# Stacked halves of q and k placed by DMA, outputs of a pair of heads added at once, reciprocals for three blocks at once

## The chip, the cores and the metric

The kernel runs on one core of one Trainium2 chip. The metric is the device time of one execution in microseconds (us).

## What is computed

Two transformer blocks on 512 rows of width 1024 in float32, the output of the first being the input of the second. The first is one layer with three branches of 8 heads of 64 each: A is attention with a relative bias, B a gated recurrence, C attention with a part of q and k turned by position. The second has two layers, each with 8 heads of forgetting attention, 8 heads of retention, a gated convolution and a gated extra input. Of all this the change touches the heads:

```python
def forgetting_attention(q, k, v, f_logit):
    ...
        logits = jnp.einsum('bhqd,bhkd->bhqk', qb, k).astype(jnp.float32) * scale
        logits = logits + cq[..., :, None] - cum[..., None, :]
        qpos = start + jnp.arange(Q_BLOCK)
        logits = jnp.where(kpos[None, :] <= qpos[:, None], logits, -jnp.inf)
        probs = jax.nn.softmax(logits, axis=-1)
        return jnp.einsum('bhqk,bhkd->bhqd', probs.astype(v.dtype), v)

def chunkwise_retention(q, k, v, log_gamma):
    ...
        scores = jnp.einsum('bhid,bhjd->bhij', qc, kc) * intra_decay
        inner = jnp.einsum('bhij,bhje->bhie', scores, vc)
        cross = jnp.einsum('bhid,bhde->bhie', qc, state) * q_decay[:, :, None]
```

Branch A's heads are the forgetting heads with a bias by distance in place of the decay and a mask by chunks of 64; the kernel computes retention over all 512 rows at once, with a table of decays over the lower triangle.

## The kernel before

**Layout.** Activations are held as channels x rows: a tile is 128 x 512, 128 channels (two heads) by all 512 rows. Every float32 operand of a matmul is split into a high half of type fp32r (a rounded copy) and a low half (what is left), and a product takes three matmuls: high by high, low by high, high by low. The dense products (`lin`, line 503; the tile is `lin` in the profile) do this with 128 x 512 outputs and make up most of the work of TensorE.

**Who sets the order.** Nothing is ordered by hand. The host runs all pieces of work as generators in a planner (`Net`, line 248; `drive`, line 301), each with a priority, lower first, and the order in which they issue is the order of the program on each engine. The planner has a clock `now` of TensorE's work, which goes on with each matmul (128 x 512: 215.8 ns), and a guess of when VectorE, ScalarE and GpSimd are done with what they have (`Eng`, line 211): VectorE 75 + 1.042 ns for each column, ScalarE 100 + 0.84, GpSimd 165 + 0.84, each a bit more for operands that are one per partition. A piece that waits for an engine yields `w()`, the guessed end plus 200 ns. DMAs by SyncE have no cost in it; a piece that waits for one yields a fixed time (`HD` 3700 ns for the exchange of rows in the rotary product, `SD` 3000 ns for tables). The stream of dense products has priority 20 and fills TensorE whenever no head is due. Roles (`take`, `give`) hold back what may run at once: `Q` (2) is the number of pairs that hold stacks, `R` (2) the number of retention pairs, `S` and `T` the attention heads in their scores and in their outputs, `sc`, `po` and `pt` are the PSUM tiles of scores, outputs and transposes.

**Weights.** SyncE's queue loads weights in program order into three buffers `raw` (line 426); ScalarE makes the high half `wh`, VectorE the low half `wl`, and the next load is issued when `wl` is planned. The same queue carries, in program order, everything else that SyncE issues.

**Heads.** `heads` (line 1052) runs a pair of attention heads in A and in the layers, `ret` (line 1716) a pair of retention heads, `hgrn` (line 1250) a pair of branch B. For both kinds of q and k that stand as a pair in one tile, `stack` (line 802, 20 times: 4 in A, 8 in each layer) builds three operands for each head e of the pair: `qd` has the high half of q in both blocks of 64 partitions, `ks` has the high half of k in the head's own block and the low half in the other, and `ql` has the low half of q in one block and zeros in the other. So two matmuls over 128 partitions, qd by ks and ql by ks, give the scores of a head. ScalarE copies q (`qh`), half of k into `ks` and half of qh into `qd`; GpSimd copies the other half into `qd` and sets half of `ql` to zero; VectorE does four subtractions of 64 x 512. `soft` (line 865) makes the probabilities P of a block of 128 rows: bias and least value (VectorE), exponential with the sum over the row (ScalarE), reciprocal of the sum (VectorE), scaling (GpSimd). The four blocks of P are then transposed (`pt`), split into `ph` and `pl`, and `pv` (line 777) multiplies them with the values. The result po (128 x 512, in PSUM) has two parts in its two blocks of 64 partitions, which `pvout` (line 792) adds: ScalarE copies one part across the blocks (`tl`), VectorE adds it to the other, straight from PSUM, into this head's half of `y`. 56 heads do this: 8 each in A, B and C, 16 in each layer.

**The rotary product** (`rotary`, line 1692; q and k of retention pairs) writes `ra` on VectorE, exchanges its blocks of 32 partitions into `rb` by four DMAs from SyncE's queue, then multiplies `ra` on GpSimd and `rb` on VectorE by tables and adds the two on VectorE.

In the profile the operations of VectorE, ScalarE and GpSimd stand at line 221 (`Eng`), matmuls at 379, transposes at 389, loads of weights at 432, the exchange of rows at 1703. In names of tiles, `lg` is a score with its bias, `m` its least value, `st` a retention score with its decay `dec`.

Of the kernel before, what the change touches and what calls it, by code (L numbers as in the profile page):

```python
# [8 lines left out]
F32 = mybir.dt.float32  # L9
F32R = mybir.dt.float32r  # L10
# [3 lines left out]
AF = mybir.ActivationFunctionType  # L14
ALU = mybir.AluOpType
# [5 lines left out]
TUNE = dict(  # L21
    NG=66,
    NTRI=5,
    MARGIN=8,
    MQ=4,
    R=2,
    Q=2,
    S=1,
    T=1,
    LAT=200.0,  # L30
    HD=3700.0,
    SD=3000.0,
    LATPOS=3,
# [7 lines left out]
NT = S // 128  # L41
# [206 lines left out]
class Net:  # L248
# [543 lines left out]
    def pvout(self, h, po, y, yev):  # L792
        nc = self.nc
        a, b = (slice(0, 64), slice(64, 128)) if h % 2 == 0 else (slice(64, 128), slice(0, 64))
        tl = yield from self.g("tl")
        self.ac.activation(tl[a], po[b], AF.Copy)
        yield self.w("ac")
        self.dv.tensor_tensor(out=y[a], in0=po[a], in1=tl[a], op=ALU.add)
        self.free(po, tl)
        self.sig(yev, "dv")  # L800

    def stack(self, q, k):


        qh = yield from self.g("qh", F32R)
        self.ac.activation(qh, q.h, AF.Copy)
        qd, ks, ql = [], [], []
        for e in range(2):
            r, o = slice(64 * e, 64 * e + 64), slice(64 - 64 * e, 128 - 64 * e)
            ks.append((yield from self.g("ks", F32R)))  # L810
            self.ac.activation(ks[e][r], k.h[r], AF.Copy)
            ql.append((yield from self.g("ql", F32R)))
            self.pl.memset(ql[e][o].bitcast(F32), 0.0)
        yield self.w("ac")
        for e in range(2):
            r, o = slice(64 * e, 64 * e + 64), slice(64 - 64 * e, 128 - 64 * e)
            self.dv.tensor_tensor(out=ks[e][o], in0=k.h[r], in1=ks[e][r].bitcast(F32), op=ALU.subtract)
            qd.append((yield from self.g("qd", F32R)))
            self.pl.tensor_scalar(out=qd[e][r], in0=qh[r].bitcast(F32), scalar1=1.0, scalar2=1.0, op0=ALU.mult, op1=ALU.mult)
            self.ac.activation(qd[e][o], qh[r].bitcast(F32), AF.Copy)  # L820
        for e in range(2):
            r = slice(64 * e, 64 * e + 64)
            self.dv.tensor_tensor(out=ql[e][r], in0=q.h[r], in1=qh[r].bitcast(F32), op=ALU.subtract)
        self.free(qh, q.h, k.h)
        yield self.w("dv", "gp", "ac")
        return [[(qd[e], ks[e]), (ql[e], ks[e])] for e in range(2)], [[qd[0], ks[0], ql[0]], [qd[1], ks[1], ql[1]]]

    def head(self, h, qk, vs, y, yev, bias, mask, qdone, hdone):

        nc = self.nc  # L830
        yield from self.take("S", 1, TUNE["S"])
        P = yield from self.tri("P")
        po = (0, 128, 384, 768, 1280)
        pev = [Ev() for _ in range(NT)]
        for i in range(NT):
            w = 128 * (i + 1)
            ps = yield from self.psr("sc", 2, "sc")
            for j, (q, k) in enumerate(qk):
                self.mm(ps[:, :w], q[:, 128 * i:w], k[:, :w], j == 0, mask is None and j == len(qk) - 1)
            if mask is not None:  # L840
                self.mm(ps[:, 128 * i:w], self.idb, mask, False, True)
            self.spawn(self.soft(ps, w, P[:, po[i]:po[i + 1]], bias, pev[i]), 0)
            yield 300.0
# [6 lines left out]
        evs = [Ev() for _ in range(NT)]  # L850
        at = self.AT
        yield pev[NT - 1]
        for j in range(NT):
# [10 lines left out]

    def soft(self, ps, w, p, bias, ev):
        nc = self.nc
        m = self.sm(1, "m")
# [11 lines left out]
        yield self.w("dv")  # L879
        sm = self.sm(1, "sum")  # L880
        self.ac.activation(p, src, AF.Exp, bias=m, scale=-1.0, accum_out=sm)
        self.free(tmp)
        yield self.w("ac")
        r = self.sm(1, "r")
        self.dv.reciprocal(r, sm)
        yield self.w("dv")
        self.pl.tensor_scalar(out=p, in0=p, scalar1=r, scalar2=1.0, op0=ALU.mult, op1=ALU.mult)
        self.sig(ev, "gp")

# [162 lines left out]
    def heads(self, pr, q, k, vs, y, mk, mask, prio=2):  # L1052
# [6 lines left out]
        else:  # L1059
            qk, used = [[(q[e].h[q[e].s], k[e].h[k[e].s])] for e in range(2)], [[q[e].h, k[e].h] for e in range(2)]  # L1060
        t = yield from self.g("y")
        e2 = [Ev(), Ev()]
# [17 lines left out]
        yield e2[1]  # L1080
        yield from self.split(t, y)

# [167 lines left out]
    def hgrn(self, pr, q, z, gz, vs, y):  # L1250
        nc = self.nc
# [71 lines left out]
        self.give("Bl")  # L1323
        yv = yield from self.g("y")
        yev = [Ev(), Ev()]
        yield vs.ev
        for e in range(2):
            yield done[e]
            yield from self.pv(2 * pr + e, vs, hi[e], lo[e], None, yv, yev[e])
            self.free(hi[e], lo[e])  # L1330
            self.after(vs, 1)
# [384 lines left out]
    def ret(self, pr, q, k, gz, vs, y):  # L1716
# [11 lines left out]
        qk, used = yield from self.stack(q, k)  # L1728
        yv = yield from self.g("yr")
        yield max(0.0, there - self.now)  # L1730
        yev = [Ev(), Ev()]
        for e in range(2):
# [14 lines left out]
            if e:  # L1747
                self.give("Q")
            yield from self.pv(h, vs, ph, pl, evs, yv, yev[e])
            self.free(ph, pl, dec)  # L1750
# [459 lines left out]
```

## Time and profile before

| what | us |
| --- | --- |
| median of 3 runs (from, to) | 2324.69 (2324.03, 2325.5) |
| the profiled execution | 2324.91 |
| its span, first to last instruction | 2323.2 |
| TensorE (PE) busy | 2278.9 (98%) |
| VectorE (DVE) busy | 1518.4 (65%) |
| ScalarE (ACT) busy | 1067.4 (46%) |
| GpSimd (POOL) busy | 479.0 (21%) |
| mean granted TensorE clock | 0.994 of full speed |

How to read it: the span is from the first to the last instruction of the one execution that was recorded; the time of that execution also has what lies around the span. Busy is the time in which an engine executes instructions; two matmuls that overlap in the pipeline count once. PE is TensorE with its matmuls, SP is SyncE with its DMA queue. The span falls into branch A (to about 170 us), C and B (to about 500), the merging and the feed-forward of the first block (to about 940), the heads of the second block's first layer (about 1000 to 1150), its dense part (to about 1700), the second layer's heads (about 1700 to 1850) and its dense part.

### The profile page before, as it was taken

To read this page: it belongs to the slowest core of one execution; us is meant where nothing else is said; L and a number is where in the kernel's file an instruction comes from. 1 tells how busy PE (TensorE), PEld (TensorE's weight loads), DVE (VectorE), ACT (ScalarE), POOL (GpSimd) and SP (SyncE) were. 2 spreads that over 40 slices of the span, in tenths; PEclk is the share of its full clock that TensorE was granted. 3 is DMA by queue.
4 is the path that set the end of the run, shared out by engine and by line. 5 is a ranking of instruction groups with operands and counts; after the bars stand their busy time and mean duration, and the time that the engine had idled before them with its cause. 6 is when DMAs were issued, how large, how long until landed. Compare 5 with 4: busy or idle time off the path is not lost.

```text
span 2323.2 us, 29048 instructions
## 1 busy us (share of the span) xinstructions
PE 2278.9 (98%) x10810; PEld 1868.2 (80%) x10810; DVE 1518.4 (65%) x2375; ACT 1067.4 (46%) x1695; POOL 479.0 (21%) x571
## 2 busy tenths in 40 slices
PE   9999999999999999999999999999999999999998
PEld 6887877778888888887878888888887878888887
DVE  6878499976542554679975652457688866652466
ACT  4767466664322233466643331245556544332343
POOL 3523044431000002334430000002425320000012
PEclk9999999999999999999999999999999999999999
DMA  5321322123332222433333233323432332233332
GB/s 178 87 74 55 91 73 64 56 87 116 98 100 97 94 100 84 155 95 101 119 105 100 93 98 100 102 91 115 125 108 90 118 109 92 99 100 93 107 95 69
DMA packets 75727, 228.24 MB, mean 98 GB/s; under 512 B 9664, under 2 KB 15680, under 8 KB 75584
## 3 DMA queue, kind: packets, MB, share of 16 engines
q1 hardware_dynamic: 70400, 209.62, 28.2%
q0 software_dynamic: 5184, 16.75, 2.5%
q8 instruction: 85, 1.39, 0.3%
q14 instruction: 58, 0.48, 0.1%
HBM read 215.29 MB, written 6.32 MB: 95 GB/s over the span
## 4 chain that ended last, share of the span: by engine, by line
PE 87%; DVE 8%; issue 2%; POOL 1%; ACT 1%; DMA 0%; SPq 0%; POOLq 0%; DVEq 0%; ACTq 0%
PE lin L379 73%; PE v L379 5%; PE sc L379 3%; PE po L379 3%; DVE wl L221 2%; PE pt L389 2%; DVE xl L221 1%; DVE dg L221 1%; DVE eq L221 0%; DVE ks L221 0%; DVE pre L221 0%; DVE qk L221 0%; DVE ql L221 0%; DVE sl L221 0%; DVE suf L221 0%
## 5 line engine op out<-in xcount | busy, mean ns | idle before, releaser
L379 PE MATMUL lin<-xh,wh 128*128 128x512 f32 (+1 forms) x2752 | 1088.0, 395 | 0.0
L379 PE MATMUL lin<-xl,wh 128*128 128x512 f32 (+1 forms) x2752 | 1072.3, 390 | 6.7 <-DVE xl L221 6.7
L379 PE MATMUL lin<-xh,wl 128*128 128x512 f32 (+1 forms) x2728 | 1061.5, 389 | 0.0
L221 DVE TENSOR_TENSOR wl<-raw,wh 128x1024 fp32r<-128x1024 f32 (+3 forms) x391 | 468.9, 1199 | 500.8 <-PE lin L379 329.3
L221 ACT ACTIVATE wh<-raw 128x1024 fp32r<-128x1024 f32 (+4 forms) x394 | 392.4, 996 | 807.7 <-PE lin L379 659.8
L379 PEld LDWEIGHTS lin<-xl,wh 128*128 128x128 f32 x2752 | 517.3, 188 | 117.8 <-DVE xl L221 8.8
L379 PEld LDWEIGHTS lin<-xh,wh 128*128 128x128 f32 x2752 | 518.0, 188 | 105.0 <-issue 3.5
L379 PEld LDWEIGHTS lin<-xh,wl 128*128 128x128 f32 x2728 | 514.4, 189 | 96.7
L221 POOL TENSOR_TENSOR sq<-sq 128x512 f32<-128x512 f32 (+1 forms) x61 | 90.1, 1477 | 566.6 <-ACT sq L221 565.9
L221 POOL MEMSET pad<- 128x2 f32 x44 | 4.4, 99 | 586.3 <-DVE cv L221 586.3
L221 POOL TENSOR_SCALAR P<-P,r 128x128 f32<-128x128 f32 (+3 forms) x128 | 86.5, 681 | 149.3 <-DVE r L221 133.0
L221 DVE SCALAR_TENSOR_TENSOR cv<-pad,vec,cv 128x512 f32<-128x512 f32 x88 | 66.1, 752 | 40.7 <-ACT cv L221 39.0
L379 PE MATMUL v<-wh,xh 128*128 128x512 f32 x192 | 78.3, 408 | 0.7 <-POOL wh L221 0.7
L379 PE MATMUL v<-wl,xh 128*128 128x512 f32 x192 | 75.9, 395 | 3.1 <-DVE wl L221 3.1
L379 PE MATMUL v<-wh,xl 128*128 128x512 f32 x192 | 75.7, 394 | 0.0
L221 ACT ACTIVATE ph<-pt 128x512 fp32r<-128x512 f32 (+3 forms) x128 | 55.6, 435 | 42.2 <-PE pt L389 40.8
L221 DVE TENSOR_TENSOR x<-lin,x 128x512 f32<-128x512 f32 x80 | 54.6, 683 | 23.5 <-PE lin L379 23.5
L221 DVE TENSOR_TENSOR pl<-pt,ph 128x512 fp32r<-128x512 f32 (+3 forms) x128 | 60.2, 479 | 12.7 <-ACT ph L221 12.2
L221 ACT ACT_TABLE_LOAD x51 | 65.4, 1283 | 4.2 <-DVE qk L221 1.6
L221 ACT ACTIVATE P<-lg,m 128x128 f32<-128x128 f32 (+1 forms) x96 | 53.6, 558 | 28.9 <-DVE m L221 21.9
L221 ACT ACTIVATE tl<-po 64x512 f32<-64x512 f32 x56 | 33.2, 592 | 73.1 <-PE po L379 72.6
L221 DVE CUSTOM_DVE_ANT_0 lg<-sc,E 128x128 f32<-128x128 f32 (+1 forms) x96 | 45.6, 483 | 31.9 <-PE sc L379 23.1
(244 smaller groups left out, 2578.1 us busy)
## 6 DMA issues: line engine op xcount, KB each, us to landing
raw<-wup SPq DMA_DIRECT2D x88, 512.0 KB, 3.3
raw<-w SPq DMA_DIRECT2D x83, 512.0 KB, 3.6
raw<-wf SPq DMA_DIRECT2D x64, 512.0 KB, 3.3
raw<-wdn SPq DMA_DIRECT2D x32, 512.0 KB, 3.5
raw<-wv SPq DMA_DIRECT2D x22, 512.0 KB, 3.6
raw<-wpg SPq DMA_DIRECT2D x16, 512.0 KB, 3.3
raw<-wbr SPq DMA_DIRECT2D x12, 512.0 KB, 3.3
raw<-wdn SPq DMA_DIRECT2D x16, 384.0 KB, 3.1
```

The lines of the kernel that those rows point to most:

```text
L221: r = f(*a, **k)
L379: self.nc.tensor.matmul(out, l, r, start=start, stop=stop)
L389: self.nc.tensor.transpose(out, src, self.ident)
```

## The change

Three edits, and a constant for the planner.

*Stacks.* ScalarE copies all of q and all of k (two tiles `sph`), VectorE takes both low halves with full tiles (two tiles `spl`), and twelve DMAs of 64 rows from SyncE's queue place the halves: six of `sph` (both blocks of each qd, the own block of each ks), then six of `spl` (the other block of each ks, both blocks of each ql). ql has the low half of q in both blocks now, where one was zero. The second batch is issued by the planner after the subtractions, and 5000 ns (`ST`) after that the stack counts as ready.

*Outputs.* ScalarE copies both parts of po, one across the blocks into a shared tile `y.l`, one straight into `y.h`; po is then free, and the second head of the pair to come triggers one add of two full tiles on VectorE.

*Reciprocals.* The sums of the four blocks go to columns of one tile. Blocks 0 and 1 end with the exponential; block 2 takes the reciprocals of three columns at once, and the three scalings follow on GpSimd; block 3 is as before. Transposes wait for both.

```diff
+    ST=5000.0,
...
     def pvout(self, h, po, y, yev):
         a, b = (slice(0, 64), slice(64, 128)) if h % 2 == 0 else (slice(64, 128), slice(0, 64))
-        tl = yield from self.g("tl")
-        self.ac.activation(tl[a], po[b], AF.Copy)
+        if y.l is None:
+            y.l = yield from self.g("tl")
+        self.ac.activation(y.l[a], po[b], AF.Copy)
+        self.ac.activation(y.h[a], po[a], AF.Copy)
+        self.sig(yev, "ac")
+        y.s += 1
         yield self.w("ac")
-        self.dv.tensor_tensor(out=y[a], in0=po[a], in1=tl[a], op=ALU.add)
-        self.free(po, tl)
-        self.sig(yev, "dv")
+        self.free(po)
+        if y.s == 2:
+            self.dv.tensor_tensor(out=y.h, in0=y.h, in1=y.l, op=ALU.add)
+            self.free(y.l)
+            self.sig(yev, "dv")
...
     def stack(self, q, k):
-        qh = yield from self.g("qh", F32R)
-        self.ac.activation(qh, q.h, AF.Copy)
-        qd, ks, ql = [], [], []
+        h, l, qd, ks, ql = [], [], [], [], []
+        for x in (q, k):
+            h.append((yield from self.g("sph", F32R)))
+            l.append((yield from self.g("spl", F32R)))
+            self.ac.activation(h[-1], x.h, AF.Copy)
         for e in range(2):
-            r, o = slice(64 * e, 64 * e + 64), slice(64 - 64 * e, 128 - 64 * e)
             ks.append((yield from self.g("ks", F32R)))
-            self.ac.activation(ks[e][r], k.h[r], AF.Copy)
+            qd.append((yield from self.g("qd", F32R)))
             ql.append((yield from self.g("ql", F32R)))
-            self.pl.memset(ql[e][o].bitcast(F32), 0.0)
         yield self.w("ac")
-        for e in range(2):
-            r, o = slice(64 * e, 64 * e + 64), slice(64 - 64 * e, 128 - 64 * e)
-            self.dv.tensor_tensor(out=ks[e][o], in0=k.h[r], in1=ks[e][r].bitcast(F32), op=ALU.subtract)
-            qd.append((yield from self.g("qd", F32R)))
-            self.pl.tensor_scalar(out=qd[e][r], in0=qh[r].bitcast(F32), scalar1=1.0, scalar2=1.0, op0=ALU.mult, op1=ALU.mult)
-            self.ac.activation(qd[e][o], qh[r].bitcast(F32), AF.Copy)
-        for e in range(2):
-            r = slice(64 * e, 64 * e + 64)
-            self.dv.tensor_tensor(out=ql[e][r], in0=q.h[r], in1=qh[r].bitcast(F32), op=ALU.subtract)
-        self.free(qh, q.h, k.h)
-        yield self.w("dv", "gp", "ac")
+        for j, x in enumerate((q, k)):
+            self.dv.tensor_tensor(out=l[j], in0=x.h, in1=h[j].bitcast(F32), op=ALU.subtract)
+
+        def dma(out, in_):
+            self.nc.sync.dma_start(out=out.bitcast(F32), in_=in_.bitcast(F32))
+
+        rows = [(slice(64 * e, 64 * e + 64), slice(64 - 64 * e, 128 - 64 * e)) for e in range(2)]
+        for e, (r, o) in enumerate(rows):
+            for d in (r, o):
+                dma(out=qd[e][d], in_=h[0][r])
+            dma(out=ks[e][r], in_=h[1][r])
+        yield self.w("dv")
+        for e, (r, o) in enumerate(rows):
+            dma(out=ks[e][o], in_=l[1][r])
+            for d in (r, o):
+                dma(out=ql[e][d], in_=l[0][r])
+        self.free(*h, *l, q.h, k.h)
+        yield TUNE["ST"]
...
     def head(self, h, qk, vs, y, yev, bias, mask, qdone, hdone):
...
+        yield pev[NT - 2]
         yield pev[NT - 1]
...
     def soft(self, ps, w, P, po, i, sums, r, bias, pev):
...
-        self.ac.activation(p, src, AF.Exp, bias=m, scale=-1.0, accum_out=sm)
+        self.ac.activation(P[:, po[i]:po[i + 1]], src, AF.Exp, bias=m, scale=-1.0, accum_out=sums[:, i:i + 1])
         self.free(tmp)
         yield self.w("ac")
-        r = self.sm(1, "r")
-        self.dv.reciprocal(r, sm)
+        if i < NT - 2:
+            return
+        js = range(NT - 1) if i == NT - 2 else [i]
+        self.dv.reciprocal(r[:, js[0]:js[-1] + 1], sums[:, js[0]:js[-1] + 1])
         yield self.w("dv")
-        self.pl.tensor_scalar(out=p, in0=p, scalar1=r, scalar2=1.0, op0=ALU.mult, op1=ALU.mult)
-        self.sig(ev, "gp")
+        for j in js:
+            p = P[:, po[j]:po[j + 1]]
+            self.pl.tensor_scalar(out=p, in0=p, scalar1=r[:, j:j + 1], scalar2=1.0, op0=ALU.mult, op1=ALU.mult)
+        self.sig(pev[i], "gp")
```

Since the planner's costs change with these lines, the order moves too.

SyncE's queue at the first retention pairs of the first layer. Before, weights (`raw`) alternate with exchanges of rows (`rb2<-ra`):

```order
L432 DMA raw_8956<-w2 128x1024
L1703 DMA rb2_8962<-ra_8961 32x512 x4
L432 DMA raw_9034<-w2 128x1024
L1703 DMA rb2_9040<-ra_9039 32x512 x4
L432 DMA raw_9090<-w2 128x1024
L432 DMA raw_9140<-w2 128x1024
L432 DMA raw_9211<-w2 128x1024
L1703 DMA rb2_9217<-ra_9216 32x512 x4
```

And now, from the second batch of the retention pair's stack on:

```order
L433 DMA raw_9026<-w2 128x1024
L825 DMA ks_8994<-spl_8992 64x512
L825 DMA ql_8996<-spl_8989 64x512 x2
L825 DMA ks_8997<-spl_8992 64x512
L825 DMA ql_8999<-spl_8989 64x512 x2
L825 DMA qd_9058<-sph_9051 64x512 x2
L825 DMA ks_9057<-sph_9054 64x512
L825 DMA qd_9061<-sph_9051 64x512 x2
L825 DMA ks_9060<-sph_9054 64x512
L433 DMA raw_9085<-w2 128x1024
...
L1725 DMA rb2_9100<-ra_9099 32x512 x4
```

The exchange for the next pair's q (rb2_9217 before, rb2_9100 now) stands behind the twelve DMAs of the retention pair's stack, those of the next forgetting pair's stack and two weights.

VectorE's queue at the same place, around the product with the exchanged rows (`rb<-rb,rot`). Before:

```order
L221 TENSOR_TENSOR pl<-st,ph 128x128
L221 ISA lg,m<-sc,E 128x128
L221 ISA m 128x1
L221 ISA lg,m<-sc,E 128x256
L221 ISA m 128x1
L221 TENSOR_TENSOR rb_9217<-rb_9217,rot 128x512
L221 ISA lg,m<-sc,E 128x384
L221 ISA m 128x1
```

And now:

```order
L222 TENSOR_TENSOR st<-sc,dec 128x128
L222 TENSOR_TENSOR pl<-st,ph 128x384
L222 TENSOR_TENSOR pl<-st,ph 128x256
L222 TENSOR_TENSOR pl<-st,ph 128x128
L222 TENSOR_TENSOR rb_9100<-rb_9100,rot 128x512
L222 TENSOR_TENSOR st<-sc,dec 128x512
L222 TENSOR_TENSOR ra<-ra,rb_9100 128x512
L222 TENSOR_TENSOR st<-sc,dec 128x384
```

The product stood between the scores of an attention head, and stands now ahead of the `st` of the second retention head.

## Rows read from the trace of the kernel before

**Rows 1.** The page, part 1: busy us (share) and instructions by engine.

```profile
PE 2278.9 (98%) x10810; PEld 1868.2 (80%) x10810; DVE 1518.4 (65%) x2375; ACT 1067.4 (46%) x1695; POOL 479.0 (21%) x571
```

**Rows 2.** Windows: us, busy us (instructions) by engine, granted clock, DMA share, GB/s.

```profile
300.00:500.00 200.00, 186.06 (x1121) 145.34 (x1122) 186.39 (x286) 132.75 (x189) 86.30 (x67) 0.99 0.21 64
500.00:940.00 440.00, 439.97 (x1955) 363.98 (x1951) 217.04 (x264) 139.47 (x172) 34.13 (x30) 1.00 0.30 98
1050.00:1150.00 100.00, 96.42 (x499) 78.96 (x498) 92.40 (x188) 62.01 (x125) 50.24 (x58) 1.00 0.30 93
1750.00:1850.00 100.00, 96.21 (x491) 79.08 (x490) 89.21 (x183) 62.10 (x125) 47.47 (x53) 0.98 0.31 98
```

**Rows 3.** Waits of PE from 1050 to 1150 us: us in total, times, longest.

```profile
PE pt L389 <- POOL P L221: 2.0, 3, 1.3
PE po L379 <- DVE pl L221: 1.1, 2, 0.7
```

**Rows 4.** Groups by line: what the change removes or alters.

```profile
L221 DVE TENSOR_TENSOR ks<-qk,ks 64x512 fp32r<-64x512 f32 x24 | 18.9, 788 | 0.9 <-ACT ks L221 0.4
L221 DVE TENSOR_TENSOR ks<-ra,ks 64x512 fp32r<-64x512 f32 x16 | 12.9, 809 | 1.5 <-ACT ks L221 1.1
L221 DVE TENSOR_TENSOR ql<-qk,qh 64x512 fp32r<-64x512 f32 x24 | 18.4, 766 | 0.3
L221 DVE TENSOR_TENSOR ql<-ra,qh 64x512 fp32r<-64x512 f32 x16 | 11.6, 724 | 0.3
L221 POOL TENSOR_SCALAR qd<-qh 64x512 fp32r<-64x512 f32 x40 | 31.3, 783 | 29.1 <-ACT qh L221 27.5
L221 POOL MEMSET ql<- 64x512 f32 x40 | 20.8, 520 | 1.8
L221 ACT ACTIVATE qh<-qk 128x512 fp32r<-128x512 f32 x12 | 7.4, 620 | 0.0
L221 ACT ACTIVATE tl<-po 64x512 f32<-64x512 f32 x56 | 33.2, 592 | 73.1 <-PE po L379 72.6
L221 DVE TENSOR_TENSOR y<-po,tl 64x512 f32<-64x512 f32 x40 | 27.4, 685 | 9.8 <-ACT tl L221 9.3
L221 DVE RECIPROCAL r<-sum 128x1 f32<-128x1 f32 x128 | 18.8, 154 | 4.7 <-ACT P L221 4.1
```

**Rows 5.** Groups by line: an add of two full tiles in SBUF.

```profile
L221 DVE TENSOR_TENSOR xl<-y,xh 128x512 fp32r<-128x512 f32 x16 | 11.1, 695 | 0.0
```

**Rows 6.** Timeline of the SP queue: start us, us, issues.

```profile
1030.72 2.43 SPq L1703 DMA_DIRECT2D rb<-ra  x4
1035.61 0.33 SPq L432 DMA_DIRECT2D raw<-w  x1
1056.56 2.41 SPq L1703 DMA_DIRECT2D rb<-ra  x4
```

**Rows 7.** Tile rb: landing times of the DMAs that exchange halves of rows.

```profile
DMA to landing us min/median/max: 2.0/2.5/3.7
```

**Rows 8.** Timeline of ACT: copies of q and k of two retention pairs.

```profile
1041.71 0.62 ACT L221 ACTIVATE qh<-ra 128x512 fp32r<-128x512 f32 x1
1045.10 1.29 ACT L221 ACTIVATE ks<-ra 64x512 fp32r<-64x512 f32 x2 [2.77 <-DVE ra L221]
1048.80 0.63 ACT L221 ACTIVATE qh<-qk 128x512 fp32r<-128x512 f32 x1
...
1074.04 0.62 ACT L221 ACTIVATE qh<-ra 128x512 fp32r<-128x512 f32 x1
```

**Rows 9.** Timeline of PE: first scores of the same two retention pairs.

```profile
1051.38 0.39 PE L379 MATMUL sc<-qd,ks 128*128 128x512 f32 x1
...
1079.85 0.39 PE L379 MATMUL sc<-qd,ks 128*128 128x512 f32 x1
```

**Rows 10.** Timeline of DVE: the rotary product that needs the exchanged rows.

```profile
1061.34 1.24 DVE L221 TENSOR_TENSOR rb<-rb,rot 128x512 f32<-128x512 f32 x1
```

**Rows 11.** Timeline of POOL: three scalings of probabilities.

```profile
1066.16 5.93 POOL L221 TENSOR_SCALAR P<-P,r 128x256 f32<-128x256 f32 x3
```

More of the change, by code (lines that the diff above doesn't have):

```diff
@@ L834, in head @@
         pev = [Ev() for _ in range(NT)]
+        sums, r = self.sm(NT, "sum"), self.sm(NT, "r")
         for i in range(NT):
@@ L841, in head @@
                 self.mm(ps[:, 128 * i:w], self.idb, mask, False, True)
-            self.spawn(self.soft(ps, w, P[:, po[i]:po[i + 1]], bias, pev[i]), 0)
+            self.spawn(self.soft(ps, w, P, po, i, sums, r, bias, pev), 0)
             yield 300.0
@@ L863, in head, with soft @@
         hdone()
-    def soft(self, ps, w, p, bias, ev):
-        nc = self.nc
+    def soft(self, ps, w, P, po, i, sums, r, bias, pev):
         m = self.sm(1, "m")
@@ L879, in soft @@
         yield self.w("dv")
-        sm = self.sm(1, "sum")
-        self.ac.activation(p, src, AF.Exp, bias=m, scale=-1.0, accum_out=sm)
+        self.ac.activation(P[:, po[i]:po[i + 1]], src, AF.Exp, bias=m, scale=-1.0, accum_out=sums[:, i:i + 1])
         self.free(tmp)
         yield self.w("ac")
-        r = self.sm(1, "r")
-        self.dv.reciprocal(r, sm)
+        if i < NT - 2:
+            return
+        js = range(NT - 1) if i == NT - 2 else [i]
+        self.dv.reciprocal(r[:, js[0]:js[-1] + 1], sums[:, js[0]:js[-1] + 1])
         yield self.w("dv")
-        self.pl.tensor_scalar(out=p, in0=p, scalar1=r, scalar2=1.0, op0=ALU.mult, op1=ALU.mult)
-        self.sig(ev, "gp")
+        for j in js:
+            p = P[:, po[j]:po[j + 1]]
+            self.pl.tensor_scalar(out=p, in0=p, scalar1=r[:, j:j + 1], scalar2=1.0, op0=ALU.mult, op1=ALU.mult)
+        self.sig(pev[i], "gp")
     def hilo(self, ps, h, l, ev, after=None):
@@ L1060, in heads @@
             qk, used = [[(q[e].h[q[e].s], k[e].h[k[e].s])] for e in range(2)], [[q[e].h, k[e].h] for e in range(2)]
-        t = yield from self.g("y")
+        t = X(0)
+        t.s = 0
+        t.h = yield from self.g("y")
         e2 = [Ev(), Ev()]
@@ L1080, in heads @@
         yield e2[1]
-        yield from self.split(t, y)
+        yield from self.split(t.h, y)
     def branch_a(self, N, ya, C):
@@ L1323, in hgrn @@
         self.give("Bl")
-        yv = yield from self.g("y")
+        yp = X(0)
+        yp.s = 0
+        yv = yp.h = yield from self.g("y")
         yev = [Ev(), Ev()]
@@ L1328, in hgrn @@
             yield done[e]
-            yield from self.pv(2 * pr + e, vs, hi[e], lo[e], None, yv, yev[e])
+            yield from self.pv(2 * pr + e, vs, hi[e], lo[e], None, yp, yev[e])
             self.free(hi[e], lo[e])
@@ L1728, in ret @@
         qk, used = yield from self.stack(q, k)
-        yv = yield from self.g("yr")
+        yp = X(0)
+        yp.s = 0
+        yv = yp.h = yield from self.g("yr")
         yield max(0.0, there - self.now)
@@ L1748, in ret @@
                 self.give("Q")
-            yield from self.pv(h, vs, ph, pl, evs, yv, yev[e])
+            yield from self.pv(h, vs, ph, pl, evs, yp, yev[e])
             self.free(ph, pl, dec)
```

1 line of the change is left out of this document (removed).

## The prediction, made before the changed kernel was run

> **What bounds the kernel now.** I read the page's busy times first, then windows of stages, then what PE waits for, then the groups that the change touches, and last the timelines of SP, ACT, PE, DVE and POOL around one retention pair. TensorE is busy for 2278.9 of 2323.2 us [rows 1], so 44.3 us is all that anything off TensorE could give back. Where only dense layers run, nothing is left: from 500 to 940 us TensorE is busy for 439.97 of 440 us [rows 2]. The change adds and removes no matmul, so it can act only where TensorE stands still beside heads. Three windows show that [rows 2]: branch B (300 to 500 us) with 200 - 186.06 = 13.9 us of standing, the end of the first layer's heads (1050 to 1150) with 100 - 96.42 = 3.6 us, and the same place in the second layer (1750 to 1850) with 3.8 us. The last also has a mean granted clock of 0.98, which over 100 us is 2 us at most. In the same 100 us VectorE is busy for 92.4 and 89.2 us, more than it is anywhere else in a layer, and TensorE's waits there are 2.0 us for probabilities P that GpSimd scales and 1.1 us for pl of VectorE [rows 3]. So a gain there must come from VectorE's or GpSimd's queue getting shorter; branch A and branch C have no standing worth counting.
>
> The profiled execution took 2324.91 us, 0.22 us over the median of 2324.69. I sum against it and take the 0.2 us off at the end. About 0.2% (4.6 us) is what a measurement of this kernel can tell from no change.
>
> **The change part by part.**
>
> *Stacks (20 of them).* VectorE loses 40 subtractions for ks (18.9 + 12.9 = 31.8 us) and 40 for ql (18.4 + 11.6 = 30.0 us) [rows 4] and gets 40 of full tiles; a subtraction of two full tiles in SBUF takes 695 ns [rows 5], so 27.8 us. That is -34 us. GpSimd loses 31.3 us of qd and 20.8 us of memsets, -52 us [rows 4]. ScalarE has a full copy of q and four half copies today, and two full copies then; at 0.62 us each [rows 4, 8] that is 100 against 40, -37 us. SyncE gets 12 more DMAs for each stack, 240 in all.
>
> *Outputs (56 heads, 28 pairs).* VectorE's 56 adds at 685 ns (38 us) become 28 of full tiles at 695 ns (19.5 us): -19 us. ScalarE copies both parts, 56 more copies at 592 ns: +33 us [rows 4, 5]. ScalarE is busy for 62 of 100 us in the end of a layer [rows 2], so I cost them at nothing; without that cover a copy of 0.59 us would stand before the next pv of each head. The buffer po is free after ScalarE now, not after VectorE.
>
> *Reciprocals.* 128 become 64, 64 x 154 ns = -10 us [rows 4]. The scaling of the first three blocks of P starts only with the third sum; GpSimd then has three scalings in a row before the fourth.
>
> *What of this reaches TensorE.* In the 100 us at the end of a layer's heads stand about six stacks, five pairs of outputs and four attention heads. VectorE is relieved there by 6 x (4 x 0.76 - 2 x 0.695) = 9.9, by 5 x 0.675 = 3.4 and by 4 x 2 x 0.154 = 1.2 us: 14.5 of 92.4 us. The upper bound of the gain is all the standing and the clock's loss, 3.6 + 3.8 + 2.0 = 9.4 us. The lower bound is nothing, because the planner knows that VectorE has less to do and sets the matmuls closer by as much; only the part of a wait that its costs did not see can go. I take a bit over half, **-5.0 us**, because the two kinds of wait named in [rows 3] both sit behind the relieved queues. In branch B only the outputs change: 8 adds at 0.685 become 4 at 0.695 us, -2.7 us on a VectorE that is busy for 186 of 200 us [rows 2]. The order of the last pair's work moves there too, so the bounds are -2.7 and +3 (a quarter of the 13.9 us for a denser order, taken as an estimate from that row), and I take **-0.5 us**.
>
> *The new wait: SyncE.* The trace has no DMA of 64 rows within SBUF. The nearest row is the exchange of rows for the rotary product: four DMAs of 32 rows take 2.43 us of the queue, 0.61 us each; the other end is a weight load at 0.33 us [rows 6]. They land 2.5 us after issue in the median, 3.7 at most [rows 7]. I take 0.61 us, since that is a move within SBUF from one block of partitions to another, as these are. A stack then takes 12 x 0.61 = 7.3 us of SyncE, in two batches of six.
>
> (a) Are the operands late? A retention pair's first scores need nine of the twelve DMAs: 2 x 0.62 us of copies, 8 x 0.61 = 4.9 us to the start of the ninth, 2.5 us to land, 8.6 us together. The room today is 1051.38 - 1041.71 = 9.7 us for the first pair and 1079.85 - 1074.04 = 5.8 us for the second [rows 8, 9]. The planner grows it: it counted 1590 + 200 + 2432 + 200 = 4.4 us and now counts 1060 + 200 + 1216 + 200 + 5000 = 7.7 us, 3.3 us more. So 13.0 and 9.1 us against 8.6: just in time. With the longest landing (3.7 us) the tight pair would be 0.7 us late. Bounds 0 and 8 pairs x 0.4 = 3 us; I take **+0.5 us**.
>
> (b) What stands behind them in SyncE's queue? Weight loads, which have room, and the exchange of rows for the next rotary product. At the first retention pair of a layer the order on SyncE is now stack, stack of a forgetting pair, exchange. k of the first pair is ready at 1045.10 and its copy done at 1045.7 [rows 8]; from there four DMAs of its first batch (2.4), a weight (0.3), its second batch (3.7), the other stack's first batch (3.7), a weight (0.3) and its second batch (3.7) end at 1059.8, where the exchange was issued at 1056.56 [rows 6]. It then lands at 1059.8 + 3 x 0.61 + 2.5 = 1064.1. VectorE began the product with the exchanged rows at 1061.34 [rows 10], without a wait. So **VectorE would stand 2.8 us** at the head of its queue, with the st and pl of the second retention head right behind it, for which TensorE's scores and outputs wait. With 0.33 us an issue, the two stacks end before 1056, and nothing is late. Bounds 0 and 2.8 us in each of two layers; I count half, as TensorE's place is not fixed to VectorE's: **+3.0 us**.
>
> Sum: -5.0 - 0.5 + 0.5 + 3.0 = -2.0 us, 2322.9 us for a profiled execution and **2322.7 us** for the median: no change that can be told.
>
> **Rule against row.** GpSimd's three scalings of P from 1066.16 on took 5.93 us together, while VectorE ran through a dense row of operations [rows 11], and this is the wait of TensorE in [rows 3]. The Trainium skill (SBUF — State Buffer, section Who interferes with whom) says that a VectorE instruction with two SBUF inputs and a GpSimd instruction that reads SBUF exclude each other for a whole instruction. That rule speaks against one part of the change: the outputs' add had one input in PSUM and now has both in SBUF. The row of an add of two SBUF tiles says 0.695 against 0.685 us, a loss of 0.3 us over 28 adds, and that is what my sum has.
>
> **The rivals.**
>
> 1. *Slower: the SyncE queue.* If an issue costs 0.61 us or more, the exchange lands late by the whole 2.8 us in both layers and TensorE feels all of it (5.6 us), and the tight retention pairs are late by 0.4 us each (3 us), while a quarter of the gain is left (-2 us): +6.6 us, 2331 us. It decides from about 0.5 us an issue. For it: the row of [rows 6] and the room of 0.5 us in (a). Against it: the weights in the same queue show 0.33 us, and VectorE has less to do before it gets to the product, or more behind it that isn't urgent. Chance 0.24.
>
> 2. *Faster: the relief counts in full.* The 14.5 us off VectorE's 92.4 us remove nearly all standing in both layers (-7.4 to -9.4 us) and half of B's 2.7 us: about -8.5 us, 2316 us, at best 2312. For it: 92.4 us in 100 is a full queue, and TensorE waits only for its results. Against: the planner packs the order closer by the same amount. Chance 0.36.
>
> 3. *Nothing: GpSimd and VectorE lock each other.* The full adds and subtractions of two SBUF tiles meet the three scalings that now follow each other, and P is as late as before; the waits of [rows 3] stay, the rest cancels: 2324.5 us. For it: 5.93 us for three scalings. Against: 40 copies of qd on GpSimd go, and 80 subtractions become 40. This is how the rule above would work here. Chance 0.10.
>
> **How the numbers follow.** The forecast has 0.30, and with rival 3 (0.10) no change has 0.40; faster 0.36 is rival 2, slower 0.24 is rival 1. The range runs from rival 2 at its best (2312) to rival 1 with a little over its price (2332). No change, the likeliest alone, would be 2320 to 2327.
>
> **What would show it.** Right: VectorE down by some 60 us and GpSimd by some 50 us in all, 240 more issues on SyncE at about 0.6 us, standing of TensorE in the layers' last 100 us of heads down from 3.6 and 3.8 to about 2 us, a wait of VectorE for rb of one to three us in each layer. Wrong: a first matmul of scores that waits for ks or ql by more than 0.5 us, weights that wait for their load, standing in branch B that moves by more than 3 us, or an issue cost of 0.4 us or less.

## The result, and the profile after

The changed kernel takes 2352.5 us (median of 4 runs, 2350.1 to 2353.9) against 2324.8 us before: a ratio of 1.0118 with a 95% interval of 1.0103 to 1.0132, 27.7 us slower. The forecast was 2322.7 us and no change, and the range ended at 2332. The profiled execution took 2350.09 us, the fastest of the four. Its page, part 1, beside [rows 1]:

```profile
PE 2290.5 (98%) x10810; PEld 1872.8 (80%) x10810; DVE 1466.4 (62%) x2243; ACT 1057.9 (45%) x1689; POOL 429.2 (18%) x491
```

The relief came much as foreseen: VectorE is down by 52.0 us (some 60 were forecast), GpSimd by 49.8 (some 50). The span grew from 2323.2 to 2348.3 us, 25.1 us: TensorE stands for 57.8 instead of 44.3 us, 13.5 more, and the same 10810 matmuls are busy for 11.6 us longer. The granted clock accounts for about half of that: it was 0.992 in the mean against 0.994 before, so 0.008 x 2348.3 - 0.006 x 2323.2 = 4.8 us (an estimate from these four numbers). The other half was not taken apart. Where: the same windows as in [rows 2].

```profile
300.00:500.00 200.00, 184.49 (x1115) 143.79 (x1114) 181.58 (x281) 132.78 (x193) 84.84 (x67) 0.99 0.20 61
500.00:940.00 440.00, 440.00 (x1951) 364.25 (x1950) 216.23 (x263) 139.04 (x170) 35.43 (x30) 1.00 0.30 99
1050.00:1150.00 100.00, 90.91 (x446) 73.30 (x445) 72.22 (x145) 53.10 (x111) 36.37 (x38) 0.95 0.66 166
1750.00:1850.00 100.00, 91.23 (x453) 73.31 (x453) 72.89 (x147) 53.89 (x111) 35.98 (x39) 0.97 0.64 165
```

TensorE stands for 9.1 and 8.8 us in the two layers' windows, where it stood for 3.6 and 3.8, the granted clock fell to 0.95 and 0.97, and the DMA share doubled from 0.30 to 0.66. VectorE is busy for 72 instead of 92 us, so it is not the amount of its work that TensorE stands for. How late each part of the program is shows in two operations that both kernels have in the same place of the dense work, `h` in the first block and `pad` after each layer's heads (tile rb: shortest, median and longest ns, then first and last start in us). Before:

```profile
L221 DVE TENSOR_TENSOR pad<-lin,rb x44: 681/683/685, 1225.4 to 2223.2; 128x512 f32<-128x512 f32 x44
L221 DVE TENSOR_TENSOR h<-lin,rb x32: 681/683/691, 600.3 to 849.5; 128x512 f32<-128x512 f32 x32
```

And after:

```profile
L222 DVE TENSOR_TENSOR pad<-lin,rb x44: 682/683/684, 1239.6 to 2248.1; 128x512 f32<-128x512 f32 x44
L222 DVE TENSOR_TENSOR h<-lin,rb x32: 681/683/692, 601.3 to 850.6; 128x512 f32<-128x512 f32 x32
```

In these two executions the first block is 1.0 us late, the first layer's heads add 13.2 us (14.2 at the first `pad`), the second layer's 10.7 (24.9 at the last).

SyncE's queue at the place that the prediction worked out (timeline of SP: start, us, issues):

```profile
1046.10 1.13 SPq L825 DMA_DIRECT2D qd<-sph  x2
...
1050.36 0.33 SPq L433 DMA_DIRECT2D raw<-w  x1
1051.81 0.46 SPq L825 DMA_DIRECT2D ks<-spl  x1
...
1055.64 2.59 SPq L825 DMA_DIRECT2D qd<-sph  x2
...
1063.99 1.18 SPq L825 DMA_DIRECT2D ql<-spl  x2
1065.27 2.44 SPq L1725 DMA_DIRECT2D rb<-ra  x4
```

Twenty-four DMAs at about 0.59 us (14 us), two weights and some stops hold the queue for 19 us, and the exchange of rows (rb) is issued at 1065.27; in the kernel before it was issued at 1056.56 [rows 6]. The longest stop, inside the 2.59 us from 1055.64, is a wait for a landing. The trace shows how it comes about: the queue's DMAs signal eight semaphores strictly in turn, so a DMA stands until the one eight issues before it has landed, here the weight load issued at 1050.36. Waits of SP from 1050 to 1060 us:

```profile
SPq L825 <- DMA raw<-w: 2.7, 2, 1.6
```

The stacks' own DMAs land late too (tile qd: us from issue to landing):

```profile
DMA to landing us min/median/max: 2.2/4.2/7.3
```

Stretches of 3 us of the same place (PE first, granted clock, DMA share and GB/s last):

```profile
1046.00:1049.00 3.00, 3.00 (x15) 2.49 (x14) 3.00 (x6) 1.61 (x3) 0.00 (x0) 1.00 0.97 287
1052.00:1055.00 3.00, 3.00 (x15) 2.44 (x13) 1.54 (x3) 0.99 (x1) 0.00 (x0) 1.00 1.08 221
1055.00:1058.00 3.00, 0.33 (x2) 0.00 (x0) 0.61 (x2) 0.07 (x1) 0.00 (x0) 1.00 1.04 219
1058.00:1061.00 3.00, 2.34 (x5) 1.62 (x6) 0.69 (x1) 0.05 (x1) 0.00 (x0) 0.53 0.88 203
1061.00:1064.00 3.00, 3.00 (x10) 2.58 (x9) 0.70 (x2) 1.11 (x2) 0.00 (x0) 0.50 0.99 249
1064.00:1067.00 3.00, 3.00 (x14) 2.45 (x13) 2.17 (x6) 0.73 (x2) 0.00 (x0) 0.84 1.04 280
```

Three things are to be seen. The sixteen DMA engines are full (share 0.88 to 1.08). TensorE does next to nothing from 1055 to 1058. And then its clock is at the lower level, 0.5 of 2.4 GHz, until about 1065: 7 us at half the clock lose another 3.5 us, so the standing of 3 us is paid about twice. Waits from 1000 to 1160 us, of TensorE and of VectorE (us in total, times, longest):

```profile
PE sc L380 <- issue: 4.5, 2, 3.0
PE po L380 <- DVE pl L222: 2.7, 4, 1.2
PE sc L380 <- DMA ql<-spl: 2.0, 4, 0.6
DVE rb L222 <- DMA rb<-ra: 8.7, 7, 3.1
```

The word issue in the first line means that the profile names nothing that the engine waited for. In the second layer VectorE waited 10.2 us for rb, at 6 places. So two stories offered themselves: the stacks' operands come late to the scores, or the exchange comes late to VectorE. TensorE's own list, with the scores (sc) at its head, speaks for the first.

### The profile page after: what moved, and what is told of

Read it like the earlier page. It is cut to its first block, busy times and chain, and to the rows that moved or that the text cites. A ratio compares the mean times of both kernels' runs of the same rounds, so it can differ in the third digit from the quotient of the medians.

```text
span 2348.3 us, 29240 instructions
## 1 busy us (share of the span) xinstructions
PE 2290.5 (98%) x10810; PEld 1872.8 (80%) x10810; DVE 1466.4 (62%) x2243; ACT 1057.9 (45%) x1689; POOL 429.2 (18%) x491
## 4 chain that ended last, share of the span: by engine, by line
PE 83%; DVE 8%; DMA 4%; issue 2%; SPq 1%; ACT 1%; POOL 1%; POOLq 0%; DVEq 0%; ACTq 0%
PE lin L380 70%; PE v L380 6%; PE sc L380 3%; PE po L380 2%; DVE wl L222 2%; PE pt L390 1%; DMA rb<-ra 1%; DMA ql<-spl 1%; DVE xl L222 1%; SPq L1725 1%; DVE dg L222 1%; DMA qd<-sph 1%; DMA raw<-wo 1%; DVE eq L222 0%; DVE qk L222 0%
## 5 line engine op out<-in xcount | busy, mean ns | idle before, releaser
L222 POOL TENSOR_SCALAR P<-P,r 128x128 f32<-128x128 f32 (+3 forms) x128 | 81.4, 649 | 194.5 <-DVE r L222 177.6
L380 PE MATMUL po<-pl,vs 128*128 128x512 f32 x192 | 60.9, 336 | 9.8 <-DVE pl L222 9.3
```

The source lines that it names most:

```text
L222: r = f(*a, **k)
L380: self.nc.tensor.matmul(out, l, r, start=start, stop=stop)
```

## The experiments

Each ratio is to the kernel before, measured beside the run; it took 2324.1 to 2324.8 us there. Where the stacks' DMAs are left out, or bring what nobody reads, the scores are other numbers: such a kernel tells about time alone.

**Take the DMAs away, or only the wait for them.** In the first kernel the stacks' DMAs go and the scores read the copies; in the second the DMAs stay and nobody reads what they bring. In both the order of the instructions is that of the changed kernel.

```diff
# e1_no_dmas: both loops of dma(...) go; e2_dmas_unread: they stay
-        return [[(qd[e], ks[e]), (ql[e], ks[e])] for e in range(2)], ...
+        return [[(h[0], h[1]), (l[0], h[1])] for e in range(2)], ...
```

> The changed kernel without the twelve DMAs of a stack: the scores read the copies sph and spl where they are (both heads of a pair with all 128 partitions, so the scores are other numbers); the planner, its costs and the order of all other instructions stay. Theory A (the stacks' 1.5 MB fill the DMA engines, so q and k come late to the scores) and theory B (the rotary exchange of rows stands behind the stacks' issues on SyncE, so VectorE stands and pl comes late to TensorE) both give back the 13.1 and 10.8 us of the two layers: 2352.5 - 24 = about 2328 us, and a few less if VectorE's relief is worth something. Theory C (the new order of instructions is worse by itself) keeps 2345 us or more.

Measured: 2319.9 us, 0.9979 of before (0.9970 to 0.9989). The DMAs are the whole loss, and without them, were that possible with real operands, the change would be a gain. Theory C falls.

> The changed kernel with its twelve DMAs for each stack, but the scores read sph and spl as in the kernel without them (so the scores are other numbers): the DMAs fill the queue and the DMA engines as before, and nothing waits for what they bring. Theory A loses its waits (first scores of five pairs, 8.0 us in the first layer and 4.6 in the second, and the half clock behind them, some 6 us): about 2334 us. Theory B keeps the wait of VectorE for the exchange: 2345 us or more.

Measured: 2351.7 us, 1.0117 (1.0102 to 1.0132). Nothing comes back, so the operands' wait is not the price, though the changed kernel's list of waits has it first. In this run's waits from 1000 to 1160 TensorE's wait before the scores is gone, the part named issue too, and others stand in its place:

```profile
PE po L380 <- DVE pl L222: 7.6, 4, 2.9
PE po L380 <- ACT ph L222: 4.4, 1, 4.4
DVE rb L222 <- DMA rb<-ra: 16.9, 6, 9.3
```

VectorE's wait for rb doubles, 16.9 for 8.7 us: TensorE gets to the same late exchange sooner, and waits there.

**Take the exchange out of SyncE's queue.**

```diff
             for g in range(4):
-                nc.sync.dma_start(out=b[32 * g:32 * g + 32], in_=a[32 * (g ^ 1):...])
+                nc.gpsimd.dma_start(out=b[32 * g:32 * g + 32], in_=a[32 * (g ^ 1):...])
```

> The changed kernel with the rotary exchange of rows issued from GpSimd's queue instead of SyncE's, no cost of it in the planner, so the order is kept. Theory B loses its wait: VectorE's 8.7 and 10.2 us for rb go to under 4 us in each layer, and the time to about 2340 us. Theory A: the exchange still shares full DMA engines and the scores still wait for the stacks, 2347 to 2353 us.

Measured: 2337.1 us, 1.0056 (1.0041 to 1.0071): 15.5 us back, with every stack and its waits as it was. Theory B holds for half of the loss, and 17 us stay. VectorE still waits 6.2 us for rb in each layer, where under 4 was expected. TensorE is granted 0.995 of its clock here, so of the 13.7 us between the two spans (2348.3 and 2334.6) about 7 are the clock (0.008 x 2348.3 - 0.005 x 2334.6, an estimate as above).

> The exchange of rows issued from GpSimd's queue, and the stacks' DMAs unread as well (the scores read the copies where they are, so they are other numbers). With the exchange in SyncE's queue this second step gave nothing (2351.7 against 2352.5). If what is left above the kernel without the DMAs (2337.1 - 2319.9 = 17 us) is the scores' wait for their operands, this run gives it back: 2320 to 2326 us. If it is the exchange itself, slow among full DMA engines, it stays: 2332 to 2338 us.

Measured: 2337.7 us, 1.0053 (1.0039 to 1.0066). The rest is not the operands either.

> No stack DMAs (the scores read the copies where they are, so they are other numbers), and the exchange of rows from GpSimd's queue. It prices that queue by itself: with the stacks' DMAs it left 2337.1 us, 17 over the kernel without them. If that rest is the exchange slow among full DMA engines, this run is at 2319 to 2323 us. If it is GpSimd's queue, where four issues of 0.5 us and a wait for ra stand ahead of the scalings of P, it is 2328 to 2338 us.

Measured: 2321.1 us, 0.9985 (0.9976 to 0.9994). It is not GpSimd's queue: the move costs about 1 us here (2321.1 against 2319.9), which is not clear of the noise.

**Same issues, fewer bytes.** The unread DMAs move the first 256, or the first 64, of 512 columns.

```diff
-            self.nc.sync.dma_start(out=out.bitcast(F32), in_=in_.bitcast(F32))
+            self.nc.sync.dma_start(out=out[:, 0:S // 8].bitcast(F32), in_=in_[:, 0:S // 8].bitcast(F32))
```

> The kernel whose stacks' DMAs nobody reads, with each of these DMAs cut to the first 256 of 512 columns: as many issues, half the bytes (the scores read the copies where they are, so they are other numbers); the order of the instructions is the same. Theory T, the transfer: the sixteen DMA engines are full while a stack is placed (share 0.97 to 1.08 from 1046 to 1058 us in the changed kernel), so half the bytes give back most: 2322 to 2335 us. Theory I, the issue: twelve issues of 0.59 us hold SyncE whatever they move, and the exchange behind them is as late as before: 2347 to 2353 us.

> As the kernel with half the bytes, now the first 64 of 512 columns: as many issues, an eighth of the bytes, the same order (the scores read the copies where they are, so they are other numbers). Full bytes took 2351.7 us, half 2344.6, no DMAs 2319.9. Theory I (twelve issues at 0.59 us and their eight slots hold SyncE) has most of the loss left when bytes are gone: 2337 to 2343 us. Theory T (transfers) continues the line: 2351.7 - 2 x 7.1 x 0.875 = 2339 us if the rest is issue, and 2325 us or less if landing times fall faster than bytes. Under 2328 us the issues cost nothing by themselves.

Measured: 2344.6 us with half the bytes, 1.0081 (1.0068 to 1.0095), and 2343.7 us with an eighth, 1.0082 (1.0066 to 1.0097). The first lies between the ranges of theories T and I, the second just above theory I's. Bytes are worth 8 us here, all of it in the upper half as far as the noise tells. In the stretches of 3 us from 1046 to 1064 the DMA engines' share is 0.88 to 1.08 with all bytes, 0.50 to 0.90 with half and 0.16 to 0.79 with an eighth. The other 24 us stay when the engines are no longer full: they are issues. The timeline of SP with an eighth of the bytes:

```profile
1048.46 1.14 SPq L825 DMA_DIRECT2D qd<-sph  x2
...
1056.91 1.11 SPq L825 DMA_DIRECT2D qd<-sph  x2
...
1065.00 2.44 SPq L1725 DMA_DIRECT2D rb<-ra  x4
```

An issue of 16 KB takes what one of 128 KB takes; the stop of 2.59 us is gone, but the queue is still held for 16.5 us.

> The exchange on GpSimd's queue, the stacks' DMAs unread and cut to an eighth of their bytes (the scores read the copies where they are, so they are other numbers): nothing but issues is left, and the exchange is not behind them. If the 17 us left with the exchange on GpSimd's queue are transfers in full DMA engines, this run is at 2320 to 2325 us. If they are something else in SyncE's queue, such as late weights, it stays at 2332 us or more.

Measured: 2321.2 us, 0.9986 (0.9976 to 0.9995). With the exchange elsewhere, 240 issues cost nothing, and the 17 us that stayed were bytes. Waits from 1000 to 1160 us with the exchange on GpSimd, first with the full bytes (unread), then with an eighth of them:

```profile
PE po L380 <- DVE pl L222: 7.4, 9, 1.6
DVE rb L222 <- DMA rb<-ra: 7.4, 5, 3.0
```

```profile
PE po L380 <- DVE pl L222: 1.8, 3, 0.9
DVE rb L222 <- DMA rb<-ra: 2.8, 2, 2.5
```

The exchange's own DMAs, only 64 KB each, land later beside the full bytes (tile rb, first the full bytes, unread, then an eighth):

```profile
DMA to landing us min/median/max: 1.9/3.4/5.1
```

```profile
DMA to landing us min/median/max: 1.8/2.2/3.4
```

All of it in one table, us:

| exchange issued from | no stack DMAs | an eighth | half | full, unread | full, read |
| --- | --- | --- | --- | --- | --- |
| SyncE | 2319.9 | 2343.7 | 2344.6 | 2351.7 | 2352.5 |
| GpSimd | 2321.1 | 2321.2 | not run | 2337.7 | 2337.1 |

The two prices do not add up. With the exchange behind them the issues cost 24 us and the bytes 8 more; with the exchange elsewhere the issues cost nothing and the bytes 16. Whether the bytes act through the late exchange alone, or through weights and other loads too, was not tried by itself.

**The parts of the change apart.**

```diff
# e4_old_stack: stack() of before, all else changed; e8_stacks_only: stack() changed, all else of before
```

> The stack of the kernel before, with the changed outputs and reciprocals. Theories A and B: all of the loss goes, and what is left is the gain or the loss of the outputs and reciprocals, between 2318 and 2327 us. Theory C: this part of the change has a loss of its own, over 2328 us.

> The changed stacks alone, outputs and reciprocals as before. The old stack with the changed outputs and reciprocals took 2325.9 us, 1.8 over before; if the parts add up, this run takes 2352.5 - 1.8 = 2350.7 us (2348 to 2354). If the loss needs the other two parts, it is under 2340 us.

Measured: 2325.9 us for the outputs and reciprocals alone, 1.0012 (1.0003 to 1.0021), and 2353.8 us for the stacks alone, 1.0121 (1.0105 to 1.0136). The stacks are the loss by themselves.

> The kernel before with the changed outputs in branch B alone. If the changed outputs (and the order they give there) are the late branch B: 2326 to 2329 us. If not, 2323.5 to 2325.5 us.

Measured: 2326.7 us, 1.0012 (1.0003 to 1.0021): the changed outputs in branch B alone cost 2.3 us (0.7 to 4.9). In its trace the matmuls stand in the order of before outside branch B; the same ones start 2.1 us earlier than before just ahead of the changed part and 0.25 us later just behind it. Waits of TensorE from 420 to 480 us, before and in this run:

```profile
PE sc L379 <- POOL ek L221: 3.0, 1, 3.0
PE sc L379 <- DVE eq L221: 1.7, 2, 1.0
```

```profile
PE sc L379 <- POOL ek L221: 4.4, 2, 2.4
PE sc L379 <- DVE eq L221: 3.2, 2, 2.6
```

> The old stack, branch B's outputs as before, the other outputs and reciprocals as changed. With branch B changed it took 2325.9 us. If B is the loss there, 2320 to 2324 us, faster than before; if the outputs and reciprocals in the layers are worth nothing, 2324 to 2326.

Measured: 2322.5 us, 0.9994 (0.9985 to 1.0003), 3.4 us under the same with branch B changed. Outputs and reciprocals in the other heads are at best a small gain.

**Let the planner wait longer.** ST = 8000 and HD = 9000 in place of 5000 and 3700.

> The changed kernel with ST = 8000 and HD = 9000: the planner puts the scores 3 us and the product with the exchanged rows 5.3 us later, so that neither stands at the head of its queue, and TensorE has dense products meanwhile. The DMAs stay. If the loss is standing behind late DMAs (theory B and its kind), most of it goes: 2325 to 2338 us. If the DMAs take the time whatever stands behind them, 2348 us or more.

Measured: 2343.1 us, 1.0079 (1.0066 to 1.0093). This lies between the two ranges. VectorE's wait for rb is all but gone (0.2 us in the second layer), but only 9.4 us come back. From 1150 to 1250 us, where the heads end and the feed-forward begins, TensorE is busy for 93.93 us, and for 96.64 us in the run whose DMAs nobody reads: as far as the windows show, the heads, put off, end too late for what follows them. That was not tried by itself.

**Fewer DMAs, or none, with real operands.** The first kernel has four DMAs for a stack: ScalarE writes the heads' own blocks, and q's low half is one full tile for both heads; ST is 4000 there. The second has GpSimd and VectorE place the four other blocks.

```diff
+            self.ac.activation(t[0], x.h, AF.Copy)
+            self.ac.activation(t[1][64:128], x.h[64:128], AF.Copy)
...
+        dma(qd[1][0:64], qd[1][64:128])
...
+        dma(ks[0][64:128], lk[0:64])
+        dma(qd[0][64:128], qd[0][0:64])
+        dma(ks[1][0:64], lk[64:128])
...
+        return [[(qd[e], ks[e]), (lq, ks[e])] for e in range(2)], ...
```

> A stack with four DMAs of 64 rows in place of twelve: ScalarE writes the head's own blocks of qd and ks (two full copies and two of half the partitions), VectorE makes the two low halves as in the changed kernel, ql is the full tile of q's low half for both heads (its other block meets the low half of k only), and DMAs bring the four other blocks; the outputs and reciprocals as changed, ST = 4000. A third of the issues and of the bytes: both theories T and I say that little of the loss is left, 2320 to 2326 us, at best the 2319.9 us of the kernel without DMAs. Over 2330 us would say that neither amount is the cause.

Measured: 2334.9 us, 1.0040 (1.0028 to 1.0053). A third of the DMAs leaves 15 of 32.6 us, nearly half. This is a miss, and beyond the mark of 2330 us by which neither amount would be the cause. The runs with fewer bytes and with the exchange elsewhere stand against that reading: they keep the changed kernel's order, and this one does not. In its trace VectorE waits only 1.9 and 3.7 us for rb in the two layers, and TensorE waits 3.0 us for a stack's own DMA in the first (`qd<-qd`). What makes up its 15 us was not taken apart.

> A stack without DMAs: ScalarE writes qd and ks of the first head as full copies and those of the second as half copies, GpSimd copies the two other blocks of qd, VectorE takes q's low half once for both heads (a full tile, whose other block meets the low half of k only) and the two low halves of k; no memsets. Outputs and reciprocals as changed. Beside the stack before it saves one of four subtractions (0.77 us x 20), a copy on ScalarE and the memsets, with no DMA to wait for. The old stack with the same outputs took 2325.9 us, no DMAs at all 2319.9: between them, 2319 to 2325 us.

Measured: 2329.7 us, 1.0023 (1.0014 to 1.0031), a miss: less work than before on VectorE and GpSimd, no DMA, and yet slower. VectorE waited 4.7 us for rb in the first layer there. Why the planner's order comes out that way was not taken apart further.

> The stack with four DMAs, the exchange of rows on GpSimd's queue, branch B's outputs as before, the other outputs and reciprocals as changed. The four DMAs with the exchange on SyncE took 2334.9 us; its first block was 4.6 us late and its two layers 1.1. If branch B's outputs cost what e15 should show and the exchange is free of the queue: 2322 to 2328 us. Under 2322 us would be faster than both kernels.

Measured: 2322.5 us, 0.9992 (0.9983 to 1.0001). With the exchange out of the way and branch B as before, four DMAs a stack are no loss that can be told.

> The stack without DMAs and memsets (2329.7 us with the exchange on SyncE and branch B changed), the exchange of rows on GpSimd's queue, branch B's outputs as before. Branch B gives back about 2.3 us; if the exchange's place gives as much as VectorE waited for it there (4.7 and 3.5 us), 2320 to 2324 us; if not, 2326 to 2328.

Measured: 2323.4 us, 0.9995 (0.9987 to 1.0004), as expected: 6.4 us come back, of which branch B has about 2.3, and the kernel cannot be told from the one before.

> The old stack, the exchange on GpSimd's queue, branch B's outputs as before, the other outputs and reciprocals as changed. With the exchange on SyncE it took 2322.5 us. Weights alone are beside the exchange in SyncE's queue there, so nothing should change: 2321 to 2324 us.

Measured: 2329.8 us, 1.0025 (1.0014 to 1.0035), a miss by 6 us. The exchange on GpSimd's queue was free where the stacks had been taken off GpSimd; with the old stack's copies and memsets in that queue, GpSimd is busy for 61 instead of 51 of 100 us at the end of the first layer's heads, and the move costs 7 us. That GpSimd's fuller queue is the reason was not tried by itself. Of the versions that place real operands, none can be told from the kernel before as faster.

## Why the prediction was wrong

**The bound** was right: the change acts beside the heads, in both layers, and dense work did not move (440.00 of 440 us from 500 to 940).

**The relief (-5.0 us)** was right in kind and rather low. Without the DMAs the kernel is 4.2 us faster than before (0.9979, so 2.6 to 7.0), and that with branch B's 2.3 us against it. In the layers TensorE then hardly stands at all (first layer's window, no DMAs, beside [rows 2]):

```profile
1050.00:1150.00 100.00, 99.70 (x521) 82.93 (x520) 86.75 (x172) 62.05 (x126) 35.88 (x40) 1.00 0.35 108
```

The two operations that mark the places of the program show by how much (no DMAs):

```profile
L222 DVE TENSOR_TENSOR pad<-lin,rb x44: 683/684/685, 1224.2 to 2215.6; 128x512 f32<-128x512 f32 x44
L222 DVE TENSOR_TENSOR h<-lin,rb x32: 682/684/692, 602.8 to 852.0; 128x512 f32<-128x512 f32 x32
```

Against before, the first block is 2.5 us late in this execution, the first layer then gains 3.7 us and the second 6.4. That is 10.1 us, a little over the upper bound of 9.4.

**Branch B (-0.5 us)** was +2.3 us, of the other sign, though inside its bounds of -2.7 and +3. TensorE waits longer there although VectorE has 2.7 us less to do. The changed order is the likely reason; it was not tried by itself.

**The issue cost (0.61 us)** was right: 0.59 us in the trace.

**Late operands (a), +0.5 us**, was right in size by luck. "Just in time" was wrong: they land after 4.2 to 4.4 us in the median, not 2.5, and TensorE does wait for them, up to 3 us at once. But taking that wait away gave 0.8 us with the exchange on SyncE and nothing with it on GpSimd, neither clear of the noise; by the lists of waits, TensorE then stood for the late exchange in its place.

**The exchange behind the stacks (b), +3.0 us**, is the step that failed. The exchange behind the issues was a right mechanism, and rival 1 had it as the slower case at 6.6 us; but its size was wrong, and the bytes were missing beside it. The DMAs cost 2352.5 - 2319.9 = 32.6 us, of which 24 stay with an eighth of the bytes. Four things were wrong in the sum. It counted one exchange in each layer, the one at the first retention pair; VectorE waited for rb at 7 and 6 places, 8.7 and 10.2 us. It had the queue free at 1059.8 where it was free at 1065.2: its 14 us for the two stacks were 19, since it counted only four of the first six DMAs and no stops. [rows 7] is a landing time beside weights, and there was no term for DMA engines that are full (12 x 128 KB for each stack), which stop the queue itself through late landings, as at 1055.64, and slow the small exchange. Bytes are 8 us of the loss with the exchange on SyncE, and 16 with it on GpSimd. It halved the price since TensorE's place is not fixed to VectorE's, where st and pl of the retention heads stand behind the product. And it had no term for the clock: about 5 of the 25.1 us of the span, at the lower level after TensorE stood; the prediction counted the clock as a possible gain of 2 us and not as a loss. The range, which allowed rival 1 little over its price, was too narrow for a cost whose nearest row was a single exchange in an idle queue.

**Rival 3** did not decide: the changed outputs outside branch B, with the reciprocals, cost nothing that can be told (2322.5 us). But its row was there. The full add of the outputs took 926 ns in the mean of the 20 in `y` (820 for the 8 in `yr`), not 695, 5.6 us in all where the sum had 0.3. Five of the six slow ones (1.70 to 1.78 us) stand beside the rotary product on GpSimd; beside the scalings of P an add stays fast (timelines of DVE and of POOL):

```profile
1118.61 0.73 DVE L222 TENSOR_TENSOR yr<-yr,tl 128x512 f32<-128x512 f32 x1
1143.01 1.78 DVE L222 TENSOR_TENSOR y<-y,tl 128x512 f32<-128x512 f32 x1
```

```profile
1118.27 2.56 POOL L222 TENSOR_SCALAR P<-P,r 128x128 f32<-128x128 f32 x4 [5.92 <-DVE m L222]
1142.63 1.62 POOL L222 TENSOR_TENSOR ra<-ra,rot 128x512 f32<-128x512 f32 x1 [10.62 <-DMA rb<-ra]
```

The Trainium skill (SBUF — State Buffer, section Who interferes with whom) says that a VectorE instruction with two SBUF inputs contends with a GpSimd instruction that reads SBUF. This trace agrees for the rotary product of two tiles (1.78 us for an add of 0.69) and not for the scaling of P, beside which the add took 0.73 us. The other adds are no clean case: one took 1.10 us beside a scaling of `E`, and three in branch B took 0.68 us with a product beside them for half a microsecond.

## What to carry to other kernels

Before small moves are given to a DMA queue, list what else stands in that queue with a due time, count every such transfer, and price issues (here 0.59 us each whatever the bytes) and bytes against the engines' share separately; the two need not add up. What the engine that bounds the kernel waits for at one place need not be the price: take that wait away and see whether the time follows. And price a standing of TensorE with the slower matmuls that come after it.

## What was not expected of the hardware

A DMA of 64 rows within SBUF takes 0.59 us of its queue for 128 KB and for 16 KB alike. Stacks of twelve with 128 KB each bring the share of the sixteen DMA engines to about 1 at 200 to 290 GB/s, land after 4.2 us in the median (7.3 at most), and slow a 64 KB exchange from another queue from 2.2 to 3.4 us (2.9 in the run whose scores read them). The queue's DMAs signal eight semaphores in turn, so that a late landing stops the issue eight places behind it. A standing of 3 us of TensorE was followed by about 7 us at half the clock.
